# Splitting the first adaLN weight slabs by feature tile, and moving the second tile's loads, products and modulation

## The chip, the cores and the metric

The kernel runs on one core of one Trainium2 chip. Its time is the device time of one execution in microseconds (us), the median of several runs; the kernel before takes 650.75 us (three runs, 649.06 to 651.46). The profile is one more execution, taken by the hardware profiler, with a time of its own. Times in the text are counted from the start of the span, the stretch from the first to the last instruction.

## The reference, cut to what matters

One layer of a diffusion backbone on x (1024 tokens by 1024 features) with 256 context tokens:

```python
shift, scale, gate = adaln(c, w_ada, b_ada)          # silu(c) @ w_ada + b_ada, split in three
shift_c, scale_c, gate_c = adaln(c_ctx, w_ada, b_ada)
h = rmsnorm(x, norm_g) * (1 + scale) + shift
hc = rmsnorm(ctx, norm_g) * (1 + scale_c) + shift_c
q, k, v, za, u, bg, cg, zc = split(h @ w_in)          # w_in is 1024 x 4096
attn = neighbourhood_attention(q, k, v, kc, vc, rpb) * silu(za)
conv = gated_short_conv(u, bg, cg, zc)
out = x + gate * (concat(attn, conv) @ w_out)
```

The change concerns only the start: the two columns `silu(c)` and `silu(c_ctx)` times the shift and scale parts of `w_ada`, the normalisation of x, and the first products of h with `w_in` (three of the eight column groups, for the convolution).

## The kernel before, in words

**Tiles.** Features are cut into eight tiles of 128 (`KT` = 8, index k), tokens into eight tiles of 128 (index t) and two halves of four tiles each. A feature tile of h is kept transposed, features on partitions and 1024 tokens along the row, as a high and a low fp32r part (`hh[k]`, `hl[k]`). A product with full accuracy takes three matmuls: high by high, low weight by high, high weight by low.

**Order.** Up to the output stage the order of the instructions on each engine is written out by hand (`strict`): each engine, and SP's queue of loads too, runs its instructions in the order of the program text, and a waiting instruction holds up all behind it on the same engine.

**Loads at the start** (lines 527 to 555, all issued by SP). `load_slab(m, j)` loads the columns of `w_ada` for the two feature tiles 2m and 2m + 1; j = 0 is the shift part, j = 1 the scale part. A slab is 1 MB: 128 partitions by 8 rows of 256 numbers (1 KB runs). For m = 0 each of the two slabs comes as two DMAs of 512 KB. `load_x` loads token tiles of x, 512 KB each in 4 KB runs. `load_chunks` loads 192 KB of `w_in` for one feature tile k, in 512 byte runs. The order before is: slab (0,0), slab (0,1), x tiles 0 to 3, chunk 0, x tiles 4 to 7, chunk 1, slab (1,0), slab (1,1), chunks 2 and 3, slab (2,0). Later slabs share three buffers, so that a load can wait for a slab's last reader.

**Modulation.** `products(m, j)` (line 594) multiplies the two columns `c2` with a slab into a PSUM tile `tr`, two rows of 512 results; a plain fp32 matmul is two instructions in the trace. `row_copy` (ACT) brings the rows to SBUF, `modulation` (line 611) turns them to columns by tiny matmuls, and three small DVE operations make the shift and scale columns `ab`.

**Normalisation of x.** `square(t)` on ACT sums the squares of a token tile, `root(t)` is an addition on DVE and a power on POOL, `norm(t)` scales the tile on DVE. In the text `norm(t)` of one tile stands ahead of `root(t + 1)` or just behind it.

**From x to h.** `transposed(half, k)` (PE) turns the four token tiles of a half for feature tile k into one of two PSUM buffers `tr`; `turn(half, k, on)` (line 651) applies the modulation: ACT makes the high part, ACT or DVE the full value `hw`, DVE the low part. `split_chunk(k)` makes the high (ACT) and low (DVE) part of a chunk. `first_columns(half, k, part)` (line 670) is the product, nine matmuls of 512 columns in three parts: part 0 needs the high parts, part 1 the chunk's low part, part 2 h's low part. The accumulators `acc0[u][half]` take six PSUM banks and `tr` the other two.

**The order around the change** (lines 718 to 778): both slab products, the squares and norms of tiles 0 to 3, one modulation for feature tiles 0 and 1, the transposes of the first half for k = 0 and 1, `first_columns(0, 0)` and `(0, 1)` with the norms of tiles 4 to 7 beside them, half of `products(1, 0)`, `transposed(1, 0)`, the rest of `products(1, 0)`, `transposed(1, 1)`, `products(1, 1)`, `first_columns(1, 0)`, `row_copy(1)`, `transposed(0, 2)`, `modulation(1)`, `turn(0, 2)`, the splits of slab pair 2, `first_columns(1, 1)`; then a loop over m.

Of the kernel before, what the change touches and what calls it, by code (L numbers as in the profile page):

```python
# [19 lines left out]
P = 128  # L20
# [19 lines left out]
def body(tc, es, x, ctxt, w_ada, b_ada, w_in, q_g, k_g, rpbr, w_out, vecs, cst, out):  # L40
# [100 lines left out]
    def place(k, shape, dtype, name):  # L141

        return hpool.tile(shape, dtype, name=name, tag=f"h{k}")
# [377 lines left out]
    def tr():  # L521
        return ps0.tile([P, 512], F32, name="tr", tag="tr", bufs=2)
# [4 lines left out]
    def load_x(ts):  # L527
        for t in ts:
            xx[t] = xp.tile([P, D], F32, name="xx", tag="xx", bufs=8)
            sp.dma_start(xx[t], x[0, t * P:(t + 1) * P])  # L530

    def load_slab(m, j):

        new = place(6 + j, [P, KT, 256], F32, "slab") if m == 0 else sl.tile([P, KT, 256], F32, name="slab", tag="slab", bufs=3)
        n = 2 if m == 0 else 1
        for i in range(n):
            rows = slice(KT // n * i, KT // n * (i + 1))
            sp.dma_start(new[:, rows], bass.AP(w_ada.tensor, w_ada.offset + j * D + 256 * m + 3 * D * P * rows.start,
                                               [[3 * D, P], [3 * D * P, KT // n], [1, 256]]))
        slabs[m, j] = new  # L540

    def load_chunks(ks):
        for k in ks:
            chunks[k] = chunk_load(CU, k)

    load_slab(0, 0)
    load_slab(0, 1)
    load_x(range(4))
    load_chunks([0])
    load_x(range(4, 8))  # L550
    load_chunks([1])
    load_slab(1, 0)
    load_slab(1, 1)
    load_chunks([2, 3])
# [3 lines left out]
    for u, half in (0, 0), (2, 0), (0, 1), (2, 1), (1, 0), (1, 1):  # L558
        acc0[u][half] = ps0.tile([P, 512], F32, name=f"acc{u}{half}", tag=f"acc{u}{half}")

    pv = tr()
    pe.transpose(pv[:, :nvec], vec[:nvec], ident[:nvec, :nvec])
    dve.tensor_copy(vecT, pv[:, :nvec])
    act.activation(c2[:].rearrange("p k a -> p a k"), vecT[:, 0:16].rearrange("p (a k) -> p a k", a=2), AF.Silu)
# [7 lines left out]
    def square(xtile, n):  # L572

        sqj = cvp.tile([P, D], BF16, name="sqj", tag="cu", bufs=1)
        sums[n] = xp.tile([P, 1], F32, name="xss", tag="xss", bufs=4)
        act.activation(sqj, xtile, AF.Square, scale=1.0 / 32, accum_out=sums[n])

    def root(n):
        dve.tensor_scalar(sums[n], sums[n], EPS, None, ALU.add)
        pool.tensor_tensor(sums[n], sums[n], mhalf[:, 0:1], ALU.pow)  # L580

    def norm(xtile, n):
        dve.tensor_scalar(xtile, xtile, sums[n], None, ALU.mult)
# [10 lines left out]
    def products(m, j, kts=range(KT)):  # L594

        if m not in mods:
            mods[m] = tr()
        rows = mods[m][:2 if m < 2 else 4, 256 * j:256 * j + 256]
        parts = [(c2, slabs[m, j])] if m < 2 else [(c4, highs[j]), (c4, lows[j])]
        for i, (c, part) in enumerate(parts):  # L600
            for kt in kts:
                pe.matmul(rows, c[:, kt], part[:, kt], start=(i == 0 and kt == 0 and j == 0),
                          stop=(i == len(parts) - 1 and kt == KT - 1 and j == 1), skip_group_check=True)

    def row_copy(m):
        n = 2 if m < 2 else 4
        rw = cvp.tile([4, 512], F32, name="rw", tag="ub", bufs=2)
        act.copy(rw[:n], mods[m][:n])
        return rw[:n]

    def modulation(m, rw):

# [32 lines left out]
    def transposed(half, k, ts=range(4)):  # L645
        if (half, k) not in pts:
            pts[half, k] = tr()
        for i in ts:
            pe.transpose(pts[half, k][:, i * P:(i + 1) * P], xx[4 * half + i][:, k * P:(k + 1) * P], ident)

    def turn(half, k, on):

        modulated(rows_of(hh[k], half), rows_of(hl[k], half),
                  pts.pop((half, k))[:].rearrange("p (r b c) -> p r b c", r=8, b=8), k, 0, on)
# [58 lines left out]
    def split_chunk(k):  # L713
        chunks[k] = chunk_split(chunks[k])

    more_h(range(6))

    products(0, 0)
    products(0, 1)
    for t in range(4):  # L720
        square(xx[t], t)
    root(0)
    root(1)
    norm(xx[0], 0)
    root(2)
    norm(xx[1], 1)
    root(3)
    norm(xx[2], 2)
    rw = row_copy(0)
    modulation(0, rw)  # L730
    norm(xx[3], 3)
    transposed(0, 0)
    transposed(0, 1)
    square(xx[4], 4)
    root(4)
    split_chunk(0)
    turn(0, 0, dve)
    square(xx[5], 5)
    norm(xx[4], 4)
    root(5)  # L740
    turn(0, 1, dve)
    first_columns(0, 0)
    square(xx[6], 6)
    norm(xx[5], 5)
    root(6)
    square(xx[7], 7)
    norm(xx[6], 6)
    root(7)
    split_chunk(1)
    norm(xx[7], 7)  # L750
    first_columns(0, 1)
    products(1, 0, range(4))
    transposed(1, 0)
    turn(1, 0, act)
# [1 line left out]
    load_slab(2, 1)  # L756
    load_chunks([4, 5])
    transposed(1, 1)
    products(1, 1)
    load_slab(3, 0)  # L760
    split_chunk(2)
    turn(1, 1, act)
    first_columns(1, 0)
    rw = row_copy(1)
    split_chunk(3)
    split(2, 0, 0)
    load_slab(3, 1)
    load_chunks([6, 7])
    transposed(0, 2)
    modulation(1, rw)  # L770
    turn(0, 2, dve)
    split(2, 0, 1)
# [1 line left out]
    split(2, 1, 1)  # L774
    xc = sl.tile([P, 2, D], F32, name="xc", tag="slab", bufs=3)
    sp.dma_start(xc, ctxt[0].rearrange("(i p) d -> p i d", p=P))
    first_columns(1, 1)
    transposed(1, 2)

    for m in range(1, 4):  # L780
# [251 lines left out]
    def both(v, n, pair):  # L1032

        w = 256 if n % 4 == 0 else 384
        return v[:, pair[0][0]:pair[-1][0] + 1, :w]
# [387 lines left out]
```

## Time and profile before

| what | value |
|---|---|
| median of the runs (649.06 to 651.46) | 650.75 us |
| the profiled execution's own time | 651.68 us |
| its span | 649.9 us |
| mean granted TensorE clock | 0.994 |
| DVE busy | 431.9 us, 66% of the span |
| ACT busy | 322.6 us, 50% of the span |
| POOL busy | 129.4 us, 20% of the span |
| DMA traffic | 125.46 MB, 193 GB/s over the span |

The engines are PE (TensorE's matmuls), PEld (its weight loads), DVE (VectorE), ACT (ScalarE), POOL (GpSimd) and SP, which issues loads. The profile's page gives each engine's busy time, then the span in 40 slices (about 16 us each) with a busy digit in tenths. The chain of waits follows the work that ended last backwards, so that each piece of it held up the next. The timeline lists instructions as "start, duration, engine, line, operation, written tile <- read tiles, shape, count", with the idle time before it and what ended that in square brackets. Line 55 is the wrapper that records all instructions, so work is told apart by its tiles: `tr<-slab,c` are the slab products, `tr<-ci,rw` the modulation's tiny matmuls, `tr<-ci,xx` the transposes, `acc<-h,wh` and `acc<-h,wl` the matmuls of `first_columns`, `sqj<-xx` a square, `xss` the two steps of a root, `xx<-xx,xss` a norm, `h<-tr,ab` the high part in `turn`, `hw` its full value, `h<-hw,h` its low part.

### The profile page before, as it was taken

The numbers are of one execution on the slowest core, as the hardware profiler recorded it, in microseconds if no ns is written. First come the engines' busy times: TensorE is split into PE (matmuls) and PEld (weight loads), VectorE is DVE, ScalarE is ACT, GpSimd is POOL, SyncE is SP. The second block draws the span as 40 slices with busy tenths as digits, with TensorE's granted clock in tenths as the row PEclk, the third lists the DMA queues.
The fourth block names the chain that finished last, engine by engine and source line by source line (L and its number), as shares of the span: only waits on it lengthen the run. The fifth ranks groups of instructions, "written<-read, shape, count | busy, mean of one in ns | idle before, by whom it ended". The sixth has DMA issues, their size and how long they took to land.

```text
span 649.9 us, 10273 instructions
## 1 busy us (share of the span) xinstructions
PE 629.0 (97%) x3469; PEld 539.2 (83%) x3469; DVE 431.9 (66%) x814; ACT 322.6 (50%) x693; POOL 129.4 (20%) x137
## 2 busy tenths in 40 slices
PE   5799999999999999999999999999999999999997
PEld 1467799899899999977877888888888888888885
DVE  1557774966684856457786889988998864575111
ACT  3466653442553635428677558565685645352000
POOL 1203203312222132101121111111211111004321
PEclk9799999999999999999999999999999999999999
DMA  8854637686686898789939576886782223966521
GB/s 321 314 179 166 168 105 243 202 263 196 196 278 177 251 262 254 187 228 218 241 103 238 145 179 191 211 213 153 207 190 75 74 75 118 324 222 222 178 102 50
DMA packets 118864, 125.46 MB, mean 193 GB/s; under 512 B 32817, under 2 KB 89353, under 8 KB 117532
## 3 DMA queue, kind: packets, MB, share of 16 engines
q1 hardware_dynamic: 112348, 113.23, 60.9%
q10 hardware_dynamic: 6208, 11.05, 5.3%
q0 software_dynamic: 256, 0.54, 0.3%
q8 instruction: 27, 0.44, 0.3%
q14 instruction: 25, 0.20, 0.1%
HBM read 88.01 MB, written 38.53 MB: 195 GB/s over the span
## 4 chain that ended last, share of the span: by engine, by line
PE 72%; DMA 7%; DVE 7%; ACT 5%; SPq 4%; issue 2%; POOL 1%; ACTq 0%; DVEq 0%; POOLq 0%
PE pu L55 22%; PE pacc L55 17%; PE po L55 5%; PE pout L74 4%; PE pout L75 4%; PE pout L76 4%; SPq L55 3%; PE tr L55 3%; PE cacc L55 3%; PE pss L55 2%; PE pmx L55 2%; DMA v<-v_d 2%; DMA k_s<-k_d 2%; PE pc L55 2%; DVE mx L55 2%
## 5 line engine op out<-in xcount | busy, mean ns | idle before, releaser
L55 PE MATMUL pu<-h,uh 128*128 128x512 f32 x544 | 169.0, 392 | 0.0
L55 PE MATMUL pacc<-wh,h 128*128 128x384 f32 x512 | 135.1, 338 | 0.0
L55 PEld LDWEIGHTS pu<-h,uh 128*128 128x128 f32 x544 | 98.2, 188 | 17.0
L55 PE MATMUL pu<-h,ul 128*128 128x512 f32 x272 | 106.3, 391 | 0.0
L55 PEld LDWEIGHTS pacc<-wh,h 128*128 128x128 f32 x512 | 92.9, 188 | 0.1
L55 POOL TENSOR_TENSOR plc<-sc,phc 128x512 fp32r<-128x512 f32 x32 | 42.5, 1328 | 221.9 <-ACT sc L55 113.2
L55 PE MATMUL pacc<-wl,h 128*128 128x384 f32 x256 | 85.6, 335 | 0.0
L55 POOL TENSOR_TENSOR ss<-ss,few 128x4 f32<-128x4 f32 (+1 forms) x40 | 42.0, 1051 | 126.9 <-DVE ss L55 126.5
L55 PEld LDWEIGHTS pu<-h,ul 128*128 128x128 f32 x272 | 51.1, 188 | 11.2
L55 DVE TENSOR_TENSOR mx<-mx,sb 128x384 f32<-128x384 f32 (+1 forms) x64 | 55.1, 869 | 2.0
L75 PE MATMUL pout<-wol,yh 128*128 128x512 f32 x128 | 49.8, 389 | 0.0
L76 PE MATMUL pout<-woh,yl 128*128 128x512 f32 x128 | 49.6, 389 | 0.0
L74 PE MATMUL pout<-woh,yh 128*128 128x512 f32 x128 | 48.3, 389 | 0.0
L55 PEld LDWEIGHTS pacc<-wl,h 128*128 128x128 f32 x256 | 48.1, 188 | 0.1
L55 DVE TENSOR_REDUCE ss<-sq 128x4 f32<-128x260 f32 (+1 forms) x40 | 15.7, 393 | 46.0 <-ACT sq L55 45.0
L55 ACT COPY mg<-pmx 128x256 f32<-128x256 f32 x32 | 12.0, 374 | 57.8 <-PE pmx L55 47.2
L55 ACT ACTIVATE sq<-pacc 128x256 f32<-128x256 f32 x32 | 12.3, 386 | 53.1 <-PE pacc L55 52.3
L1355 DVE TENSOR_TENSOR ot<-pout,gate 128x512 f32<-128x512 f32 x16 | 10.8, 688 | 40.2 <-PE pout L76 37.7
L55 DVE TENSOR_TENSOR pll<-sb,phl 128x768 fp32r<-128x768 f32 (+2 forms) x33 | 29.3, 889 | 7.9 <-ACT sb L55 7.9
L1356 POOL TENSOR_TENSOR ot<-ot,xr 128x512 f32<-128x512 f32 x15 | 19.6, 1315 | 68.6 <-DVE ot L1355 67.6
L55 DVE TENSOR_TENSOR sc<-sc,mg 128x512 f32<-128x512 f32 x32 | 21.8, 683 | 17.1 <-ACT mg L55 17.1
L55 ACT ACTIVATE qn<-pacc,ss 128x64 f32<-128x64 f32 x128 | 30.1, 330 | 6.0 <-POOL ss L55 3.2
(146 smaller groups left out, 1276.0 us busy)
## 6 DMA issues: line engine op xcount, KB each, us to landing
uraw<-in_w_in SPq DMA_DIRECT2D x34, 256.0 KB
q_d<-qs SPq DMA_DIRECT2D x64, 128.0 KB
k_s<-k_d SPq DMA_DIRECT2D x16, 512.0 KB
q_s<-q_d SPq DMA_DIRECT2D x32, 256.0 KB
wr<-in_w_in SPq DMA_DIRECT2D x40, 192.0 KB
slab<-in_w_ada SPq DMA_DIRECT2D x6, 1024.0 KB
t_d<-btw SPq DMA_DIRECT2D x8, 576.0 KB
bt<-t_d SPq DMA_DIRECT2D x8, 576.0 KB
```

Source lines behind the costliest of these rows:

```text
L55: i = emit(*a, **kw)
L74: i = pe.matmul(ps, ah, bh, start=first, stop=False)
L75: pe.matmul(ps, ah, bl, start=False, stop=False)
L76: pe.matmul(ps, al, bh, start=False, stop=last)
L1355: dve.tensor_tensor(ot, ps, gate[:, cols], ALU.mult)
L1356: (dve if (nh, t) == (1, NB - 1) else pool).tensor_tensor(ot, ot, xr, ALU.add)
```

## The change

The slabs of feature tiles 0 and 1 are no longer one pair of 256 columns. `load_first_slabs(k)` loads, for one feature tile, the shift and the scale part as two DMAs of 512 KB in 512 byte runs. The pair of k = 0 stays first; x tiles 0 to 3 and chunk 0 follow; then the pair of k = 1, chunk 1, and x tiles 4 to 7.

`first_products(k, j)`, `first_row(k)` and `first_modulation(k)` do products, copy and modulation for one feature tile, into accumulator banks of the second half that are not yet in use (`acc0[1 - k][1]`) instead of `tr`; each plain fp32 matmul now has 128 columns instead of 256, and there are twice as many.

In the hand-written order the transposes of the first half are issued token tile by token tile. The products of k = 1 stand between the transposes of token tiles 2 and 3, and the modulation of k = 1 inside `first_columns(0, 0)`. `turn(0, 1)` follows there, with `split_chunk(1)` moved ahead of the squares of tiles 5 to 7 and of the norms of tiles 4 to 7. Further on, `products(1, 1)` with the load behind it moves behind `first_columns(1, 0)`, and part 0 of `first_columns(1, 1)` moves ahead of `modulation(1)`.

```diff
--- before.py
+++ after.py
@@ -531,24 +531,29 @@
 
     def load_slab(m, j):
 
-        new = place(6 + j, [P, KT, 256], F32, "slab") if m == 0 else sl.tile([P, KT, 256], F32, name="slab", tag="slab", bufs=3)
-        n = 2 if m == 0 else 1
-        for i in range(n):
-            rows = slice(KT // n * i, KT // n * (i + 1))
-            sp.dma_start(new[:, rows], bass.AP(w_ada.tensor, w_ada.offset + j * D + 256 * m + 3 * D * P * rows.start,
-                                               [[3 * D, P], [3 * D * P, KT // n], [1, 256]]))
+        new = sl.tile([P, KT, 256], F32, name="slab", tag="slab", bufs=3)
+        sp.dma_start(new, bass.AP(w_ada.tensor, w_ada.offset + j * D + 256 * m,
+                                  [[3 * D, P], [3 * D * P, KT], [1, 256]]))
         slabs[m, j] = new
+
+    def load_first_slabs(k):
+
+        both = place(6 + k, [P, 2, KT, P], F32, "slab")
+        for j in range(2):
+            sp.dma_start(both[:, j], bass.AP(w_ada.tensor, w_ada.offset + j * D + P * k,
+                                             [[3 * D, P], [3 * D * P, KT], [1, P]]))
+        slabs[k] = both
 
     def load_chunks(ks):
         for k in ks:
             chunks[k] = chunk_load(CU, k)
 
-    load_slab(0, 0)
-    load_slab(0, 1)
+    load_first_slabs(0)
     load_x(range(4))
     load_chunks([0])
+    load_first_slabs(1)
+    load_chunks([1])
     load_x(range(4, 8))
-    load_chunks([1])
     load_slab(1, 0)
     load_slab(1, 1)
     load_chunks([2, 3])
@@ -558,7 +563,7 @@
     for u, half in (0, 0), (2, 0), (0, 1), (2, 1), (1, 0), (1, 1):
         acc0[u][half] = ps0.tile([P, 512], F32, name=f"acc{u}{half}", tag=f"acc{u}{half}")
 
-    pv = tr()
+    pv = acc0[0][1]
     pe.transpose(pv[:, :nvec], vec[:nvec], ident[:nvec, :nvec])
     dve.tensor_copy(vecT, pv[:, :nvec])
     act.activation(c2[:].rearrange("p k a -> p a k"), vecT[:, 0:16].rearrange("p (a k) -> p a k", a=2), AF.Silu)
@@ -607,6 +612,30 @@
         rw = cvp.tile([4, 512], F32, name="rw", tag="ub", bufs=2)
         act.copy(rw[:n], mods[m][:n])
         return rw[:n]
+
+    def first_products(k, j):
+
+        ps = mods[k] = acc0[1 - k][1]
+        for kt in range(KT):
+            pe.matmul(ps[:2, P * j:P * j + P], c2[:, kt], slabs[k][:, j, kt], start=(j == 0 and kt == 0),
+                      stop=(j == 1 and kt == KT - 1), skip_group_check=True)
+
+    def first_row(k):
+        rw = cvp.tile([4, 512], F32, name="rw", tag="ub", bufs=2)
+        act.copy(rw[:2, :256], mods[k][:2, :256])
+        return rw[:2]
+
+    def first_modulation(k, rw):
+
+        pm = mods.pop(k)
+        for j in range(2):
+            pe.matmul(pm[:, 2 * j:2 * j + 2], rw[:, P * j:P * j + P], comb[:2], start=(j == 0), stop=(j == 1),
+                      skip_group_check=True)
+        both = lambda v: v[:, k:k + 1].broadcast_to([P, 2])
+        abk = ab[:, k].rearrange("p (w j) -> p j w", j=2)
+        dve.tensor_tensor(abk[:, 0], pm[:, 0:2], both(bsh), ALU.add)
+        dve.tensor_tensor(abk[:, 1], pm[:, 2:4], both(b1), ALU.add)
+        dve.tensor_tensor(abk[:, 1], abk[:, 1], both(ng), ALU.mult)
 
     def modulation(m, rw):
 
@@ -715,40 +744,54 @@
 
     more_h(range(6))
 
-    products(0, 0)
-    products(0, 1)
-    for t in range(4):
-        square(xx[t], t)
+    first_products(0, 0)
+    first_products(0, 1)
+    square(xx[0], 0)
     root(0)
+    square(xx[1], 1)
     root(1)
     norm(xx[0], 0)
+    transposed(0, 0, [0])
+    transposed(0, 1, [0])
+    square(xx[2], 2)
     root(2)
     norm(xx[1], 1)
+    rw = first_row(0)
+    first_modulation(0, rw)
+    transposed(0, 0, [1])
+    transposed(0, 1, [1])
+    square(xx[3], 3)
     root(3)
     norm(xx[2], 2)
-    rw = row_copy(0)
-    modulation(0, rw)
+    split_chunk(0)
     norm(xx[3], 3)
-    transposed(0, 0)
-    transposed(0, 1)
+    transposed(0, 0, [2])
+    transposed(0, 1, [2])
+    first_products(1, 0)
+    transposed(0, 0, [3])
+    turn(0, 0, dve)
+    transposed(0, 1, [3])
+    first_products(1, 1)
+    first_columns(0, 0, (0,))
+    rw = first_row(1)
     square(xx[4], 4)
     root(4)
-    split_chunk(0)
-    turn(0, 0, dve)
+    first_columns(0, 0, (1,))
+    first_modulation(1, rw)
+    first_columns(0, 0, (2,))
+    turn(0, 1, dve)
+    split_chunk(1)
     square(xx[5], 5)
     norm(xx[4], 4)
     root(5)
-    turn(0, 1, dve)
-    first_columns(0, 0)
     square(xx[6], 6)
     norm(xx[5], 5)
     root(6)
+    first_columns(0, 1)
     square(xx[7], 7)
     norm(xx[6], 6)
     root(7)
-    split_chunk(1)
     norm(xx[7], 7)
-    first_columns(0, 1)
     products(1, 0, range(4))
     transposed(1, 0)
     turn(1, 0, act)
@@ -756,17 +799,18 @@
     load_slab(2, 1)
     load_chunks([4, 5])
     transposed(1, 1)
-    products(1, 1)
-    load_slab(3, 0)
     split_chunk(2)
     turn(1, 1, act)
     first_columns(1, 0)
+    products(1, 1)
+    load_slab(3, 0)
     rw = row_copy(1)
     split_chunk(3)
     split(2, 0, 0)
     load_slab(3, 1)
     load_chunks([6, 7])
     transposed(0, 2)
+    first_columns(1, 1, (0,))
     modulation(1, rw)
     turn(0, 2, dve)
     split(2, 0, 1)
@@ -774,7 +818,7 @@
     split(2, 1, 1)
     xc = sl.tile([P, 2, D], F32, name="xc", tag="slab", bufs=3)
     sp.dma_start(xc, ctxt[0].rearrange("(i p) d -> p i d", p=P))
-    first_columns(1, 1)
+    first_columns(1, 1, (1, 2))
     transposed(1, 2)
 
     for m in range(1, 4):
```

## The prediction, as put on record before the result was known

> **What bounds the kernel now.** I read the page first, then the idle time at the start, because the change lies in the first 45 us.
>
> ```profile
> PE 629.0 (97%) x3469; PEld 539.2 (83%) x3469; DVE 431.9 (66%) x814; ACT 322.6 (50%) x693; POOL 129.4 (20%) x137
> ...
> PE   5799999999999999999999999999999999999997
> ```
>
> PE is busy 97% of the span, and its only poor slices are the first two, of some 16 us each. A change here can win little more than idle time of the first 32 us; what comes later follows PE. The next view is the table of stretches: start:end, length, busy time of PE, PEld, DVE, ACT and POOL, granted clock, DMA share, GB/s.
>
> ```profile
> 9.00:13.00 4.00, 4.00 (x18) 1.50 (x17) 0.15 (x1) 1.46 (x3) 0.18 (x1) 1.00 1.04 423
> 13.40:16.80 3.40, 1.65 (x8) 0.48 (x6) 2.16 (x6) 3.20 (x7) 2.29 (x3) 1.00 1.05 407
> 16.80:20.20 3.40, 2.29 (x16) 1.80 (x16) 1.95 (x7) 2.27 (x5) 1.50 (x2) 1.00 1.03 401
> 20.20:23.70 3.50, 3.38 (x8) 2.71 (x9) 3.33 (x6) 3.47 (x7) 0.55 (x1) 0.51 1.09 384
> 23.70:27.10 3.40, 1.78 (x6) 0.85 (x6) 2.31 (x6) 0.89 (x3) 1.23 (x2) 1.00 1.11 372
> 27.10:30.50 3.40, 3.40 (x9) 1.67 (x8) 0.75 (x1) 0.00 (x0) 0.05 (x1) 0.50 0.74 263
> 60.00:70.00 10.00, 10.00 (x68) 7.70 (x65) 7.25 (x10) 6.26 (x11) 7.31 (x8) 1.00 0.23 79
> 72.00:74.00 2.00, 2.00 (x12) 1.67 (x11) 0.75 (x2) 1.00 (x3) 0.00 (x0) 1.00 1.15 344
> ```
>
> Two things are to be seen. PE waits between 13.4 and 27.1 us, and it also runs at half clock twice, from 20.2 to 23.7 and from 27.1 to 30.5. Each half-clock stretch is about 3.4 us long and follows such a stretch with gaps (2.29 us busy, mostly transposes and tiny matmuls, and 1.78 us); but 1.65 us busy before 16.8 us cost nothing, so the edge is not sharp here. Loads run at 423 GB/s while x's 4 KB runs come, and at 344 with chunks alone (512 byte runs). The third view is the chain of waits (start, length, what held up the next).
>
> ```profile
> 26.80 2.70 PE acc L55 x6
> 29.50 8.87 PE tr L55 x40
> 38.37 2.28 PE acc L55 x9
> ...
> 43.41 2.83 ACT slabh L55 x3
> ...
> 47.64 2.03 PE tr L55 x16
> ```
>
> From 26.80 to 42 us PE's own work is the chain; then it goes through the modulation of the second slab pair, `turn(0, 2)`, three splits and `turn(1, 2)` on ACT to the products at 47.64, from where PE runs on without idle (10.00 of 10.00 us in the row of 60 to 70). So the change is worth what it moves **the start of that modulation**, the tiny matmuls at 41.02. The rest comes from rows of single instructions. First loads and products in the timeline of all engines:
>
> ```profile
> 6.02 9.03 PE L55 MATMUL tr<-slab,c 128*2 128x256 f32 x32 [2.44 <-DMA slab<-in_w_ada]
> ...
> 10.14 4.40 PEld L55 LDWEIGHTS tr<-slab,c 128*2 128x2 f32 x21 [0.20 <-issue]
> 11.33 1.06 ACT L55 ACTIVATE sqj<-xx 128x1024 bf16<-128x1024 f32 x1 [7.01 <-DMA xx<-in_x]
> ...
> 17.02 1.06 ACT L55 ACTIVATE sqj<-xx 128x1024 bf16<-128x1024 f32 x1 [0.26 <-DMA xx<-in_x]
> ```
>
> The slab products start as soon as the first piece of slab is there; tiles 0 and 4 of x are each waited for by their squares. Then PE's timeline where the second half begins and at the modulation:
>
> ```profile
> 31.76 0.66 PE L55 MATMUL tr<-ci,xx 128*128 128x128 f32 x4
> ...
> 41.02 1.05 PE L55 MATMUL tr<-ci,rw 2*128 2x2 f32 x8
> ```
>
> **The change part by part.**
>
> *Loads.* Bytes stay the same; 1.05 MB of slab moves behind x tiles 0 to 3 and chunk 0. The rate of 1 KB runs lies between 344 and 423 GB/s; I take 385, near the 384 of 20.2 to 23.7, when such slabs come. Tile 0 of x lands 1.05 MB earlier, 2.7 us, and loses 0.3 because the megabyte still ahead of it has 512 byte runs at 344: it lands at 11.33 - 2.4 = 8.9 us. Tile 4 landed at 17.02 behind 4.5 MB and half a megabyte of its own, so those 4.5 MB were in by 15.8; the same 4.5 MB now end with the second pair's scale slab: 15.8, plus 0.6 for 2.1 MB in short runs, is 16.4, and its shift slab is in 1.5 us before, at 14.9. Tile 4 lands at 18.2, behind chunk 1 too; slab (1,0) comes about 0.6 us later, long before its use. SP issues as many loads as before (four slab DMAs then, four now), and no issue waits for a buffer. [...]
>
> *First tile.* The views of single tiles give count, shortest, median and longest (ns), and first and last start:
>
> ```profile
> L55 ACT ACTIVATE sqj<-xx x8: 1046/1057/1058, 11.3 to 23.0; 128x1024 bf16<-128x1024 f32 x8
> L55 ACT ACTIVATION_READ_ACCUMULATOR sqj<-xx x8: 186/187/195, 12.3 to 24.0; 128x1 f32 x8
> ```
>
> ```profile
> L55 POOL TENSOR_TENSOR xss<-xss,few x8: 550/729/1032, 12.8 to 26.4; 128x1 f32<-128x1 f32 x8
> L55 DVE TENSOR_SCALAR xx<-xx,xss x8: 745/753/754, 14.0 to 27.2; 128x1024 f32<-128x1024 f32 x8
> ```
>
> ```profile
> L55 ACT COPY rw<-tr x3: 558/575/575, 16.2 to 53.6; 2x512 f32<-2x512 f32 x2, 4x512 f32<-4x512 f32 x1
> ```
>
> A square with its readout takes 1.25 us, so those of tiles 0 to 2 start at 8.9, 10.2 and 11.5. The row copy (0.57 us for 512 numbers; between nothing and 0.57 for 256, and I take 0.4) now stands ahead of square 3, which runs from 13.1 to 14.35. DVE's addition for tile 3 stands ahead of norm 2, so norm 2 (0.75) ends at 15.2; norm 3 waits for POOL's power (up to 1.03) and ends at 16.5. The first tile's modulation, its transposes and chunk 0's split fit between.
>
> *Second tile's products.* They cannot start before transposes of token tile 2, at 15.55. PE's queue is in order, so from here everything for feature tile 0 waits behind them too. One 256 column instruction took 0.21 us at full clock (4.40 us for 21), and 0.37 before (the first 11 in 4.1 us), so that the burst began at half clock. For 128 columns the bounds are half of that, 0.105, and no gain at all, 0.21; the transposes' 0.66 for four, 128 columns wide, put it near half, so I take 0.105. Two lots of 16 instructions are 3.4 us, with four transposes in between 0.3: at full clock the products end at **E = 19.3**, and the scale slab (16.4) is there in time. At half clock the 32 instructions take 6.8 us.
>
> *What follows E, at full clock.* DVE's timeline has the first tile's steps and the norms of tiles 5 and 6:
>
> ```profile
> 19.04 0.55 DVE L55 TENSOR_TENSOR wl<-wr,wh 128x384 fp32r<-128x384 f32 x1
> 20.30 0.81 DVE L55 TENSOR_SCALAR hw<-tr,ab 128x512 f32<-128x512 f32 x1 [0.71 <-ACT h L55]
> 21.14 0.69 DVE L55 TENSOR_TENSOR h<-hw,h 128x512 fp32r<-128x512 f32 x1
> ...
> 24.59 0.14 DVE L55 TENSOR_SCALAR xss<-xss 128x1 f32<-128x1 f32 x1
> 25.46 0.75 DVE L55 TENSOR_SCALAR xx<-xx,xss 128x1024 f32<-128x1024 f32 x1 [0.73 <-POOL xss L55]
> 26.13 0.15 DVE L55 TENSOR_SCALAR xss<-xss 128x1 f32<-128x1 f32 x1
> ```
>
> Row copy 0.4, beside it two parts of `first_columns(0, 0)` at 0.76 each (2.28 for nine matmuls), then half the tiny matmuls (0.55 of 1.05), three small DVE operations 0.5: the second tile's modulation is ready at E + 2.55. High part, full value and low part in `turn(0, 1)` take 2.3 us (ACT's 0.7 ahead of DVE in the bracket, then 20.30 to 21.83), chunk 1's low part 0.55. Only now come norms 4 to 7: norm 0.75, then three turns of addition, power and norm at 1.54 us each (24.59 to 26.13). Norm 7 thus ends at E + 10.8, and the second half's transposes start at E + 10.9. PE has too little to do meanwhile: its queue ends some 2.2 us before. **Here a new wait takes the old one's place**: before, the transposes at 31.76 waited for PE alone, since norm 7, the last of the norms, started at 27.2 and was over at 27.9; with E = 19.3 they start at 30.2, not earlier.
>
> *From there to the modulation.* Before: 41.02 - 31.76 = 9.26 us. `products(1, 1)` and `first_columns(1, 0)` only change places; part 0 of `first_columns(1, 1)` now lies ahead, 0.76, so 10.0. Behind the modulation the chain on ACT is the same, so that part 0 shortens nothing there but fills PE's wait. The moved load of slab (3,0) starts some 2 us later, behind `products(1, 1)`; its split comes after `turn(1, 2)`, around 48 us, which is cover enough for one megabyte.
>
> *Sum.* At full clock all through, the modulation starts at 19.3 + 10.9 + 10.0 = 40.2 against 41.02: **0.8 us gained**. But between 11.7 us (the first tile's products start at 6.0, run at half clock until 10.1 and at 0.105 us for the last 13) and 15.55 PE has only six transposes and four tiny matmuls. The rows above show half clock after such a stretch, and the next 3.4 us then fall on the second products: at most 1.7 us lost, 1.3 with an uneven fit, E = 20.6. The 2.2 us wait before the second half's transposes can do the same again, 1.7 us if it falls so; I count a quarter, 0.4. Then 41.9: **0.9 us lost**. On the profiled execution that is 651.7 + 0.9 = 652.6; the profile's execution lies 0.9 above the median shown, so beside the median the forecast is **651.6 us**.
>
> **The rivals.**
>
> 1. *The norms are not last* (faster). If DVE and POOL go through norms 4 to 7 sooner than 1.54 us each, PE bounds: it is through at E + 8.7, so 2.2 us earlier, and with full clock the modulation starts at 38.0, 3.0 us earlier: 647.7, a few tenths lower if the turns of `first_columns` close up as well. For it: POOL's powers took from 0.55 to 1.03 us for the same shape, so that part of a turn is loose. Against it: DVE's queue puts the norms behind chunk 1's split. Chance 0.12.
>
> 2. *Half clock nearly throughout* (slower). The place is 13 to 34 us; it decides once no 3.4 us stretch there has PE busy for more than about half. Price: 3.4 us on the products, 2.0 on `first_columns` and tiny matmuls ahead of the modulation's end, less what is already in the forecast, 1.7: 3.7 above it, 655.3. For it: products, then 0.9 and 2.2 us waits, look like 23.7 to 27.1 before, which lost the clock. Against it: the products themselves are dense, as those of 6 to 10 us, which ended at full clock. [...] Chance 0.18.
>
> 3. *The change does nothing*: loads are earlier, but the start waits for the second slab pair and the norms, and clock losses before and after are equal. 650.8, chance 0.10.
>
> **How the numbers follow.** The forecast has the other 0.60. A measurement of this kernel can tell about 0.5%, 3.25 us, from no change. Faster by more needs rival 1 with all its gain: 0.10. Slower by more is most of rival 2: 0.15. Within: 0.75. The range takes in all full clock with a little of rival 1, 648.2, up to just under rival 2, 655.0; about 0.1 is left out on either side. It also holds the unknown costs: 128 columns without gain (3.4 us, like half clock) and loads 0.5 us off.
>
> **What would show it.** Tile 0's square at 8.9 us (loads). The second products at 15.5 to 16 and their end at 19.3 or 20 to 21 with the clock row at half between (clock). Norm 7 ending 10.8 us behind that, PE idle before the second half's transposes at 30 to 32 (the new wait). The modulation of slab pair 1 at 40 to 42, the products behind it 6.6 us later, as before. I am wrong if those transposes come well before 30 us, or if PE idles again after 50 us where it did not.

## The result and the profile after

| | before | after |
|---|---|---|
| median of ten runs each on one chip | 650.39 us (649.06 to 652.26) | 654.97 us (652.21 to 657.92) |
| ratio, 95% interval | | 1.0063 (1.0045 to 1.008) |
| the profiled execution and its span | 651.68 us, 649.9 us | 656.41 us, 653.4 us |
| mean granted clock | 0.994 | 0.997 |
| products of slab pair 2 start | 47.64 us | 49.15 us |

The change costs 4.6 us where 0.9 was forecast. The time lies at the very edge of the range (655.0), and the sign is the forecast's, but most of the loss came from places that the prediction had called settled, so that the time lies in the range by luck. Two lines of the page of after:

```profile
PE 629.0 (96%) x3501; PEld 540.4 (83%) x3501; DVE 432.7 (66%) x817; ACT 322.9 (49%) x694; POOL 129.6 (20%) x137
...
PE   4899999999999999999999999999999999999997
```

PE's busy time is the same 629.0 us, in 32 matmuls and 32 weight loads more (3501 for 3469 each). So what the span has grown by is idle time of PE, and the digits don't show where. Mark the 64 instructions more; they matter below. The table of stretches of after (start:end, length, busy time of PE, PEld, DVE, ACT and POOL, granted clock, DMA share, GB/s):

```profile
5.40:10.40 5.00, 5.00 (x32) 3.18 (x32) 0.00 (x0) 0.93 (x1) 0.00 (x0) 1.00 0.98 356
10.40:12.80 2.40, 0.07 (x1) 0.00 (x0) 0.99 (x3) 2.19 (x5) 1.17 (x2) 1.00 1.04 383
12.80:15.20 2.40, 1.48 (x8) 0.92 (x8) 1.89 (x8) 2.03 (x6) 1.95 (x3) 1.00 1.15 346
15.20:18.60 3.40, 3.25 (x15) 1.91 (x16) 1.29 (x3) 0.00 (x0) 0.51 (x1) 0.50 1.08 403
18.60:22.00 3.40, 3.40 (x26) 2.29 (x25) 1.50 (x2) 1.39 (x3) 0.00 (x0) 1.00 1.03 405
60.00:70.00 10.00, 10.00 (x66) 7.85 (x65) 7.32 (x9) 5.80 (x10) 7.34 (x9) 1.00 0.04 19
76.00:78.00 2.00, 1.06 (x8) 0.70 (x6) 0.96 (x2) 1.63 (x4) 0.00 (x0) 1.00 0.52 150
```

Of these rows one is at half clock, 15.2 to 18.6, and it lies just on the first lot of the second products. PE is full at 60 to 70 us, as before. But at 76 to 78 it is busy for 1.06 of 2 us. That last row is the new thing. Then the start in PE's timeline of after:

```profile
5.37 5.10 PE L55 MATMUL acc<-slab,c 128*2 128x128 f32 x32 [1.84 <-DMA slab<-in_w_ada]
12.86 0.44 PE L55 MATMUL tr<-ci,xx 128*128 128x128 f32 x2 [2.39 <-DVE xx L55]
...
15.97 3.18 PE L55 MATMUL acc<-slab,c 128*2 128x128 f32 x16
...
19.45 1.91 PE L55 MATMUL acc<-slab,c 128*2 128x128 f32 x16
21.29 0.96 PE L55 MATMUL acc<-h,wh 128*128 128x512 f32 x3
...
30.27 0.66 PE L55 MATMUL tr<-ci,xx 128*128 128x128 f32 x3
32.14 0.33 PE L55 MATMUL tr<-ci,xx 128*128 128x128 f32 x1 [1.21 <-DVE xx L55]
...
41.69 1.05 PE L55 MATMUL tr<-ci,rw 2*128 2x2 f32 x8
...
49.15 1.09 PE L55 MATMUL tr<-slabh,c 128*4 128x256 f32 x8 [1.21 <-ACT hw L55]
```

The second products end at 21.3 (E), the modulation of slab pair 1 starts at 41.69 (41.02 before), and the products of slab pair 2 at 49.15 (47.64 before).

**Where the time went.** I matched the instructions of DVE and ACT in the two traces one by one and read the shift of each. It grows in steps: +0.67 us at the modulation, +0.84 between it and the products of slab pair 2, +1.35 near 72 us, +0.42 near 104, +0.25 near 345. That is 3.53 us, and the spans differ by 3.5. The rest of the two executions' 4.7 us lies outside the span (3.0 us against 1.8).

**The step of 0.84 us.** DVE's timeline, before and then after, around the three small operations (`ab`) that end the modulation:

```profile
40.38 1.22 DVE L55 TENSOR_TENSOR slabl<-slab,slabh 128x1024 fp32r<-128x1024 f32 x1 [0.39 <-ACT slabh L55]
42.10 0.16 DVE L55 TENSOR_TENSOR ab<-tr,vecT 128x4 f32<-128x4 f32 x1 [0.50 <-PE tr L55]
```

```profile
42.48 1.23 DVE L55 TENSOR_TENSOR slabl<-slab,slabh 128x1024 fp32r<-128x1024 f32 x1 [0.39 <-ACT slabh L55]
43.63 0.15 DVE L55 TENSOR_TENSOR ab<-tr,vecT 128x4 f32<-128x4 f32 x1
```

Before, the low part of a slab's split was over before the tiny matmuls were, and DVE waited 0.50 us for PE. After, it starts 2.1 us later, the `ab` operations stand behind it with no wait of their own, and they start 1.94 us behind the first tiny matmul instead of 1.08. The cause is one place further up: `products(1, 1)` ended at 38.4 and now ends at 40.5, ACT's row copy waits for it, and the splits behind the copy come later too. The row copy before and then after:

```profile
38.41 0.57 ACT L55 COPY rw<-tr 2x512 f32<-2x512 f32 x1 [2.10 <-PE tr L55]
```

```profile
40.52 0.58 ACT L55 COPY rw<-tr 2x512 f32<-2x512 f32 x1 [4.15 <-PE tr L55]
```

From the last `ab` operation to the products of slab pair 2 it is 5.27 us in both.

**The step of 1.35 us.** ACT's timeline at the loads of the query chunks, before and then after, and PE's of after:

```profile
72.96 1.06 ACT L55 CAST wh<-wr 128x384 fp32r<-128x384 f32 x2 [2.09 <-DMA wr<-in_w_in]
74.60 0.91 ACT L55 CAST wh<-wr 128x384 fp32r<-128x384 f32 x2
```

```profile
74.49 0.51 ACT L55 CAST wh<-wr 128x384 fp32r<-128x384 f32 x1 [2.12 <-DMA wr<-in_w_in]
76.37 0.51 ACT L55 CAST wh<-wr 128x384 fp32r<-128x384 f32 x1 [1.36 <-DMA wr<-in_w_in]
77.46 0.91 ACT L55 CAST wh<-wr 128x384 fp32r<-128x384 f32 x2
```

```profile
77.61 0.96 PE L55 MATMUL acc<-h,wh 128*128 128x512 f32 x3 [0.94 <-ACT h L55]
```

Before, two chunks are cast one right behind the other. After, the second waits 1.36 us for its load; the high part of the next `turn` stands behind it in ACT's queue, and PE waits for that. The chunks are loaded by the same instructions from the same place in both kernels, 192 KB each, far from anything that the diff touches. The DMA view (queue and kind: packets, MB, share of 16 engines) of two stretches of 7 us, each from 0.3 us behind the issue of the store `rope_d` that goes just ahead of these loads, before and then after:

```profile
DMA packets 2044, 1.99 MB, mean 284 GB/s; under 512 B 80, under 2 KB 1916, under 8 KB 1916
...
q1 hardware_dynamic: 2044, 1.99, 97.4%
```

```profile
DMA packets 1989, 1.98 MB, mean 283 GB/s; under 512 B 78, under 2 KB 1860, under 8 KB 1860
...
q1 hardware_dynamic: 1988, 1.96, 96.6%
q8 instruction: 1, 0.02, 0.8%
```

In after, an **instruction fetch** of 16 KB (q8) falls among the loads, and 56 packets fewer of the kernel's own queue (q1) come in the 7 us. The fetch took 0.89 us of one DMA engine. In before it comes at 79.05 us, when this burst is over. While the chunks come undisturbed, the DMA records of before have up to 352 packets in each half us (72.0 to 74.5 us), 336 to 338 of them of 512 bytes: 22 for each of 16 engines. If one engine alone lost the 56 packets, that is 1.27 us of its time, an estimate from these counts that lies near the step; the trace doesn't name the engine.

### The profile page after: what moved, and what is told of

It is laid out like the page before. It is cut to its first block, busy times and chain, and to the rows that moved or that the text cites. A ratio compares the mean times of both kernels' runs of the same rounds, so it can differ in the third digit from the quotient of the medians.

```text
span 653.4 us, 10342 instructions
## 1 busy us (share of the span) xinstructions
PE 629.0 (96%) x3501; PEld 540.4 (83%) x3501; DVE 432.7 (66%) x817; ACT 322.9 (49%) x694; POOL 129.6 (20%) x137
## 4 chain that ended last, share of the span: by engine, by line
PE 68%; DVE 9%; DMA 8%; SPq 3%; ACT 3%; issue 1%; POOL 1%; ACTq 0%; DVEq 0%; POOLq 0%
PE pu L55 20%; PE pacc L55 17%; PE po L55 5%; DMA k_s<-k_d 4%; PE pout L76 4%; PE pout L74 4%; PE pout L75 4%; PE cacc L55 3%; DVE mx L55 2%; SPq L55 2%; DVE sb L55 2%; PE pss L55 2%; PE tr L55 2%; PE pmx L55 2%; PE pc L55 1%
## 5 line engine op out<-in xcount | busy, mean ns | idle before, releaser
L55 PEld LDWEIGHTS pu<-h,ul 128*128 128x128 f32 x272 | 51.1, 188 | 11.3
L1399 DVE TENSOR_TENSOR ot<-pout,gate 128x512 f32<-128x512 f32 x16 | 10.8, 687 | 37.5 <-PE pout L76 33.2
```

What stands on the lines that cost most here:

```text
L55: i = emit(*a, **kw)
L1399: dve.tensor_tensor(ot, ps, gate[:, cols], ALU.mult)
```

## The experiments

Theory A: the loss is made at the start, by the late move of `products(1, 1)`, the wait for the norms and the clock, and what comes later follows from it or is chance. Theory B: a part is made near 72 us by something that the diff doesn't show, PE's instruction fetch, which comes earlier in the work because PE has 64 instructions more. The first eight runs split the loss among the parts; B took shape from their traces, where the step stayed whichever part was undone, and the last three runs test it. In the expectations of the first eight, theory B still says only that the later loss is a fixed consequence of the change, and in that of `norms_first` theory A is the wait for norm 7.

**The kernel after once more, and each part of the start by itself.** `after_again` is the kernel after unchanged.

> The changed kernel once more, unaltered. Theory A (the loss is made in two places: 1.5 us by the time of the products of slab pair 2, which began at 47.64 us before and at 49.15 after, and some 2 us later by single loads that land late, which differs from run to run): the first offset comes again within 1 us, depending on where the half-clock stretch falls; the second, 1.35 us at the load of the second query chunk near 75 us, comes out anywhere between 0 and 2 us. Theory B (the later loss is a fixed consequence of the change): the load near 75 us is late by 1.2 to 1.5 us again. Time by either: ratio to before 1.004 to 1.008.

Measured: 655.36 us, ratio 1.0067 (1.0044 to 1.009). The fourth transpose at 31.82, modulation 41.40, products of slab pair 2 at 48.85; the step near 72 us is 1.45. So the loss and both its places repeat.

`late_undone` puts the late moves back:

```diff
     transposed(1, 1)
+    products(1, 1)
+    load_slab(3, 0)
     split_chunk(2)
     turn(1, 1, act)
     first_columns(1, 0)
-    products(1, 1)
-    load_slab(3, 0)
...
-    first_columns(1, 1, (0,))
     modulation(1, rw)
...
-    first_columns(1, 1, (1, 2))
+    first_columns(1, 1)
```

> The changed kernel with its late part taken back: the products of slab (1,1) directly behind the transposes again, and the first product of the second half for feature tile 1 undivided behind the modulation. If part 0 ahead of the modulation costs its 0.76 us, the products of slab pair 2 start 0.8 us earlier than in the changed kernel relative to the second half's first transposes (17.0 us behind the fourth of them after; 16.2 expected here), and the time falls by about 0.8 us. If the late part is a gain, as filler for PE, they start no earlier or later. A loss that is all at the start leaves the time as in the changed kernel, 1.006.

Measured: 653.62 us, 1.0038 (1.0015 to 1.006). The products of slab pair 2 start 15.55 us behind the fourth transpose (17.01 in after, 16.2 expected). Of the 1.46 us, 0.61 lie ahead of the modulation and 0.85 behind it: the products follow it by 6.61 us, as before (6.62), and PE's wait ahead of them is back at 0.35 us. By the medians the late part is worth 1.7 us (2.87 above before, where `after_again` was 4.61 above it on the same chip), but the two intervals overlap. The step at 72 us is still 1.38, so the late part isn't what makes it. This profile has no stretch at half clock in the second products (1.91 us for each sixteen), though nothing ahead of them was changed, which may be why its start is earlier still (the products of slab pair 2 at 46.27).

`norms_first` keeps the diff and only moves the squares, roots and norms of tiles 4 to 7 up (the new places alone):

```diff
+    square(xx[4], 4)
+    root(4)
     turn(0, 0, dve)
...
+    square(xx[5], 5)
+    norm(xx[4], 4)
+    root(5)
     rw = first_row(1)
...
+    square(xx[6], 6)
+    norm(xx[5], 5)
+    root(6)
     turn(0, 1, dve)
     split_chunk(1)
+    square(xx[7], 7)
+    norm(xx[6], 6)
+    root(7)
     first_columns(0, 1)
     norm(xx[7], 7)
```

> The changed kernel with the squares and norms of token tiles 4 to 7 moved up: square 4 ahead of the first tile's turn, norm 4 ahead of the second tile's modulation, norm 5 ahead of the second turn, norms 6 and 7 behind it. Everything else as in the changed kernel. Theory A (norm 7, which ended at 32.08 us, holds up the second half's last transpose and PE waits for it): norm 7 ends near 29 us, PE goes through without a wait, the products of slab pair 2 start 1.4 us earlier, 47.7 us, ratio to before 1.003 to 1.006. Rival (the delayed second products and the half clock are all of it): norm 7 earlier, but those products no more than 0.5 us earlier.

Measured: 653.60 us, 1.0036 (1.0019 to 1.0054). Its PE timeline:

```profile
28.64 1.89 PE L55 MATMUL tr<-slab,c 128*2 128x256 f32 x8
30.46 0.66 PE L55 MATMUL tr<-ci,xx 128*128 128x128 f32 x4
```

All four transposes follow PE's own work with no bracket; the second products ran at half clock as in after (the first sixteen took 3.23 us, 3.18 in after). So the wait for norm 7 was real, and it cost 1.35 us at the modulation (40.34 against 41.69, one profile each). The step at 72 us stays, 1.42.

`pe_busy` is the kernel after with seven unread fp32 matmuls of 256 columns in PE's waits (five behind the first products, two ahead of square 3), meant to keep the clock.

> The changed kernel with seven extra plain fp32 matmuls of 256 columns whose results nothing reads, in PE's wait between the two bursts of slab products: five behind the first burst, two behind the transposes of token tile 1. If the half clock of 15.4 to 18.8 us comes from that wait, the granted clock stays at 1.0 there, the second burst ends at 19.6 instead of 21.3 us, norm 7 and the products of slab pair 2 come 1.5 us earlier, and the time falls by 1 to 1.5 us (ratio 1.004). If the clock falls from something else, it falls again, and the extra matmuls change nothing or cost up to 0.5 us.

Measured: 654.61 us, 1.0062 (1.004 to 1.0084). The clock stays at 1.00 up to the end of the second products, which end at 20.5 (19.6 expected); the fourth transpose is at 31.31, 0.8 us sooner than in after (1.5 expected). The step at 72 us is 0.7, and another, 1.4 us near 103, is larger than in after (0.42). The clock is worth 0.8 us at its place and nothing that the time can tell. All three kernels with the seven matmuls kept it here; of the profiles of the new start without them five lost it and one, `late_undone`, did not. So the matmuls are a likely reason and not a shown one.

**The late part alone, on the kernel before.** `before_again` is the kernel before unchanged, `late_alone` the same with the diff's late moves only (the last two hunks, from `products(1, 1)` on). Each was run once.

> The kernel before, unaltered, for a second profile. All five profiles with the changed start so far show a step against the first profile of before when the second query chunk is split, near 72 us (1.36, 1.47, 1.44, 1.40 and 0.73 us). Theory B (a fixed consequence of the change): this profile stays within 0.3 us of the first one there. Theory A (loads land early or late from run to run, and the first profile of before was an early one): a step of 0.7 to 1.5 us here too. The half-clock stretches may lie elsewhere in the first 35 us; the products of slab pair 2 begin between 46 and 48 us.

> The kernel before with the late part of the change alone: the products of slab (1,1) behind the first product of the second half for feature tile 0, and part 0 of that for feature tile 1 ahead of the modulation. The tiny matmuls of that modulation begin 10.0 us behind the second half's transposes instead of 9.26, and the products of slab pair 2 17.0 us behind them instead of 15.9 (within 0.3). If the late part is free, 15.9 again. At the load of the second query chunk: no step under theory B unless the late part is what causes it; 0 to 1.5 us under theory A.

Measured: 650.17 and 652.60 us. In `before_again` the transposes are at 30.33, the modulation at 39.58 and the products of slab pair 2 at 46.20: this start is 1.4 us ahead of the first profile of before. Its two stretches at half clock lie together, at 17.8 to 24.6, which may be why; no run tests it. In `late_alone` the modulation follows the transposes by 9.90 us (9.26 and 9.25 in the two profiles of before), and the products follow the modulation by 7.45 (6.62 in both). DVE's timeline of `late_alone` shows the same queue as that of after:

```profile
41.61 1.23 DVE L55 TENSOR_TENSOR slabl<-slab,slabh 128x1024 fp32r<-128x1024 f32 x1 [0.39 <-ACT slabh L55]
42.76 0.16 DVE L55 TENSOR_TENSOR ab<-tr,vecT 128x4 f32<-128x4 f32 x1
```

The late part costs 0.65 + 0.83 = 1.5 us by itself. Neither kernel has a step at 72 us (under 0.05 us in both).

**Parts together.** `both` is `norms_first` with the late moves put back; `all3` is that with the seven busy matmuls.

> The changed kernel with the norms moved up and the late part taken back. If both costs are real and add up, the products of slab pair 2 begin 0.8 us earlier than with the norms moved up alone (47.8), at 47.0 us with a half-clock stretch in the second products and near 45.5 without, so earlier than before (47.64). Time: ratio 1.000 to 1.004, since the later step near 72 us is not touched. If only one of the two costs is real, 47.6 or later and 1.004 or more.

> As the kernel with the norms moved up and the late part taken back, and the seven extra matmuls in PE's wait besides. Clock at 1.0 through 14 to 19 us in the profile, second burst over by 19.5 us, products of slab pair 2 at 45.5 us or a little before, 2 us earlier than in the kernel before. If the whole loss were at the start, that would make it faster than the kernel before by 2 us, ratio 0.997; if the loss of loads near 72 us is fixed, 0.998 to 1.001.

Measured: `both` 652.06 us, 1.0016 (0.9995 to 1.0036), with a step of 1.43 at 72 us; `all3` 651.89 us, 1.0016 (0.9991 to 1.004), with 0.17. The products of slab pair 2 start at 47.29 (47.0 expected, or 45.5 without a half-clock stretch; it had one of 6.8 us) and 45.97 (45.5 expected). With norms, late part and clock mended, the new start is only 0.2 us sooner than that of `before_again`, 46.20, so the early slabs win next to nothing there. In both, the second half's first transposes follow PE's own work without a wait (30.07 and 30.33 us).

**The fetch.** The trace's DMA records have the fetches of 16 KB one by one. By their number they are PE's: 27 in before and 28 in after for the 7039 and 7104 PE instructions of the trace, on average 250 apart, where each other engine has 1200 instructions or fewer in the whole span. The third one, and ACT's casts of the first two query chunks, in us behind the issue of the `rope_d` store:

| kernel | PE instructions more | third fetch | first cast | second cast | step at 72 us |
|---|---|---|---|---|---|
| before, before_again, late_alone | 0 | 11.74, 10.75, 11.33 | 5.65 to 5.69 | right behind | under 0.05 |
| after, after_again, late_undone | 64 | 5.42, 5.62, 5.47 | 5.67 to 5.68 | 7.56 to 7.68 | 1.35 to 1.45 |
| norms_first, both | 64 | 5.64, 5.59 | 5.68 to 5.69 | 7.65 to 7.66 | 1.42, 1.43 |
| pe_busy | 92 | 0.79 | 6.39 | right behind | 0.70 |
| all3 | 92 | 0.69 | 5.81 | right behind | 0.17 |

The step is there when the fetch falls between 5.4 and 5.7 us, and not when it falls after the burst; ahead of it, it is smaller or gone. But this was read after the fact, and most rows with the new start have the same count. So three more kernels move the fetch on purpose, by tiny fp32 matmuls of two columns that nobody reads (four instructions each), put into waits of PE at the start:

```diff
+    def tiny(n):
+        for i in range(n):
+            pe.matmul(acc0[2][1][:2, :2], c2[:, 0], c2[:, 1], start=True, stop=True, skip_group_check=True)
```

`before_64` is the kernel before with 16 of them, `after_60` the kernel after with 15, and `all3_32` is `all3` with eight. Their places in `before_64`:

```diff
+    tiny(6)
     products(0, 0)
     products(0, 1)
+    tiny(6)
...
-    first_columns(0, 1)
+    first_columns(0, 1, (0,))
+    tiny(4)
+    first_columns(0, 1, (1, 2))
```

> The kernel before, in its old order, with sixteen two-column fp32 matmuls that nobody reads put where PE waits anyway (six ahead of the slab products, six behind them, four between part 0 and part 1 of the second half's first columns). They are 64 instructions in PE's list, some 1 us of work. Theory of the instruction fetch: the third fetch of 16 KB comes 64 instructions sooner in the work, at 5.0 to 5.9 us behind the issue of the rope_d store, as in the kernel after, and not at 10.7 to 11.8; so ACT's cast of the second query chunk waits for its load, comes 1.8 to 2.1 us behind the first cast, and everything from 72 us on is 1.3 to 1.5 us later: time 1.0 to 2.0 us above before, a ratio of 1.002 to 1.003. Rival, that the 512-byte slab loads or the order of the norms make the late load: both are as in the kernel before, so no step at 72 us (under 0.1 us), and the time within 1 us of before.

Measured: 652.17 us against 651.71, 1.0016 (0.9988 to 1.0045). The fetch came 5.67 us behind the store. ACT's timeline and PE's:

```profile
71.50 0.51 ACT L55 CAST wh<-wr 128x384 fp32r<-128x384 f32 x1 [2.12 <-DMA wr<-in_w_in]
73.50 0.51 ACT L55 CAST wh<-wr 128x384 fp32r<-128x384 f32 x1 [1.49 <-DMA wr<-in_w_in]
```

```profile
74.74 0.96 PE L55 MATMUL acc<-h,wh 128*128 128x512 f32 x3 [1.06 <-ACT h L55]
```

The old order and the old loads, with 64 instructions more for PE, make the step: 1.46 us (shift against the first profile of before: -1.49 up to 68 us, -0.03 from 72). The rival expected none at that place. Nor is this an early start that a load gives back: `before_again` starts as early (-1.50 up to 68 us), its fetch comes after the burst, and its two casts stand together:

```profile
71.51 1.05 ACT L55 CAST wh<-wr 128x384 fp32r<-128x384 f32 x2 [2.14 <-DMA wr<-in_w_in]
```

> The kernel after with fifteen such matmuls (60 instructions: four ahead of the first slab products, eight behind them, three behind the first columns of the first half). Theory of the instruction fetch: the third fetch moves a further 60 instructions ahead, to before the query chunks' loads are asked for or less than 1 us behind the rope_d store; the cast of the second query chunk follows the first at once and the step at 72 us is under 0.3 us, while the start keeps its 0.7 to 1.5 us: time 1.0 to 2.0 us below after, a ratio of 1.003 to 1.005 against before. Rival, that the new order itself makes the load late: the step stays at 1.3 to 1.5 us and the time is that of after, a ratio of 1.006 to 1.007.

Measured: 655.22 us, 1.0051 (1.0025 to 1.0078). The fetch came 2.24 us ahead of the store. ACT's timeline:

```profile
74.37 1.06 ACT L55 CAST wh<-wr 128x384 fp32r<-128x384 f32 x2 [2.12 <-DMA wr<-in_w_in]
76.01 0.91 ACT L55 CAST wh<-wr 128x384 fp32r<-128x384 f32 x2
```

The two casts are together again and the step is under 0.05 us, with the start of after (products of slab pair 2 at 49.06). So theory B holds at its place, both ways. The times lean the same way and settle nothing: `before_64` is 0.5 us above before where 1.0 to 2.0 was expected, `after_60` 3.5 above where some 3.2 (4.6 less 1.4) was, and the intervals are wide enough for the rival too.

> The kernel with the late part undone, the norms ahead of the transposes and PE kept busy, and eight more two-column matmuls (32 instructions) in PE's waits at the start, so that the third fetch comes well before the query chunks' loads. Theory of the instruction fetch: no step at 72 us, the start 1.5 to 1.8 us ahead of the first profile of before; the later loads near 100 and 340 us may take back up to 2 us by where the further fetches fall: a ratio of 0.997 to 1.001. Rival, that the remainder is the 512-byte loads' own: as without the eight matmuls, 1.0016.

Measured: 651.84 us against 651.71, 0.9998 (0.9968 to 1.0028). The fetch came 1.57 us ahead of the store. No step at 72 us; the start is 1.7 us ahead of the first profile of before, and 1.4 of it is gone at 103 us. It is the best version of the new order, and no faster than the kernel before.

**What stays open.** The traces have more places where the shift jumps: at 103 us, where ACT waits for a load of `uraw` (11.3 to 13.5 us of idle time), and several between 320 and 385 us. The first runs from -0.6 to +1.6 us, the others together from -1.7 to +2.4, and the two profiles of before differ there as well (at 103 us by 1.4, which just takes back what `before_again` had won at the start). In `after_again` a stretch at half clock, 332.1 to 335.5, adds to it. By these numbers the uraw wait may swallow gains and losses made ahead of it, which would be a reason why 1.4 us at 72 us is hard to find in the time; no run here separated it. Why a fetch of 0.9 us makes a load 1.4 us late isn't settled either.

## Why the prediction was right up to the modulation and wrong behind it

- **Loads.** Tile 0's square at 9.47, forecast 8.9: the tile won 1.86 us instead of 2.4. The row of 12.80 to 15.20, when the packets are nearly all of 512 bytes (the second slabs and chunk 1), has 346 GB/s, against the 344 taken.
- **Second products.** Forecast 15.55 and E = 20.6 with a stretch at half clock; measured 15.97 and 21.3. The half-clock stretch came where it had been put. The first products ended at 10.5, where 11.7 was forecast; the forecast's own terms, 10.1 and 13 times 0.105, give 11.5. At full clock the last 16 instructions start 0.109 us apart (19.45 to 21.08), near the 0.105 taken; the start was 0.4 late. PE's longest gap ahead of the fall at 15.2 us was 2.39 us. In `after_again`, from the start of the first products on, no gap is over 0.66 us when the clock falls at 14.68 us, and in before the stretch of 16.8 to 20.2, just ahead of a half clock, has none over 0.79; so a gap of 2.39 us isn't needed. Nor does the second rival's measure, PE busy for about half of 3.4 us, decide it: in before the clock fell after 2.29 busy of 3.40 us (16.8 to 20.2) and stayed at 1.00 after 1.65 (13.4 to 16.8). What does decide it isn't shown.
- **Norm 7 at E + 10.8, and the new wait.** DVE's timeline of after:

```profile
26.70 0.75 DVE L55 TENSOR_SCALAR xx<-xx,xss 128x1024 f32<-128x1024 f32 x1
...
30.46 0.15 DVE L55 TENSOR_SCALAR xss<-xss 128x1 f32<-128x1 f32 x1
31.33 0.75 DVE L55 TENSOR_SCALAR xx<-xx,xss 128x1024 f32<-128x1024 f32 x1 [0.73 <-POOL xss L55]
```

  The last norm ends at 32.08, 10.8 us behind 21.3: right to a tenth, turn by turn (1.54 us). `norms_first` shows that it was the bound.
- **The modulation.** Forecast 41.9 in the likeliest case, measured 41.69. E was 0.7 later than forecast, and this was made good behind it: only the fourth transpose waited for norm 7, the first three began at 30.27, so that the modulation came 9.55 us behind the wait and not 10.0. No half clock came at 30 us, where 0.4 had been counted (granted clock 1.00 from 28 to 33 us).
- **First failed step: "Behind the modulation the chain on ACT is the same", the products 6.6 us behind.** They came 7.46 behind. ACT's chain itself is the same, 5.27 us from the last `ab` operation in both; what came later is those operations. I had asked what part 0 and the products do to PE and ACT, and not what the later row copy does to the splits and, through them, to DVE's queue, in which a low part of 1.23 us now stands ahead of three operations of 0.16. In `late_alone` the whole late part costs 1.5 us, where 0.76 was counted: the 0.65 ahead of the modulation had been foreseen, the 0.83 behind it had not.
- **Second failed step: from the products on, PE runs without idle and all is only shifted.** It idles at 77 us, for 1.35 us of shift, by the instruction fetch. This is what the prediction had named as the sign of being wrong. The forecast counted the instructions added to PE by their time, and they take almost none (629.0 us in both); their number moves the fetches (the third from 11.74 to 5.42 us behind the store).
- **The base.** The first profile of before had a start 1.4 us later than its repeat (47.64 against 46.20, and 46.16 in `before_64`); its second half's transposes, at 31.76, are the latest of the four profiles with the old start (30.29 to 30.93 in the others). The forecast was thus measured from a late start.
- **Rivals and chances.** No rival came true. A loss of more than 3.25 us had been given a chance of 0.15, as most of the second rival; it came by other causes. The time is close to the 655.3 us of the second rival, half clock nearly throughout, but the clock was at half for one stretch alone. A time that fits is no proof of a mechanism.

Together: the late part (1.5 us) and the wait for norm 7 (1.35) are about the 2.95 us by which the products of slab pair 2 come later in after, 49.15, than in `before_again`, 46.20; with the 1.35 to 1.45 of the fetch that is 4.3 to 4.4 us, near the 4.6 measured. Against the first profile of before the same sum gives 2.9 at 72 us. It holds to a microsecond or so at best, since the waits at 103 us and from 320 to 385 us take and give back as much. The times by themselves give most of the loss to the first two: `both`, which mends them and keeps the fetch's step, is only 0.84 us above before, and its interval (up to 1.0036) ends below that of `after_again` (from 1.0044). What the fetch adds to the whole time isn't shown: 0.5 us in `before_64` and 1.1 in `after_60`, neither clear of the noise.

## What to carry to other kernels

An edit that moves work by a microsecond must be followed through the queues of all engines that the moved work feeds, not only those of the engine that it is on: here a row copy on ACT that came 2 us later put a long operation of DVE ahead of three short ones. And when a step appears far from the edit, in code that didn't change, look at what else uses the DMA engines there; the number of instructions issued before that point, not their duration, can be what changed: here it was 64 PE instructions more, at the same 629.0 us of busy time. And a gain at one place may not last to the end: of what `before_again` had won at the start, 1.4 us was gone at the wait for `uraw` at 103 us, though it wasn't tested that this load takes it.

## What the runs showed of the hardware

- **Instruction fetches stand among the DMA records** (queue q8, kind `instruction`), in packets of 16 KB, one per some 250 PE instructions, 0.88 to 1.62 us each in before and after, 41 of 55 of them under 1.2. Where one fell 5.4 to 5.7 us behind the store, the work was 1.35 to 1.5 us late, in five kernels and one repeat; where it fell 0.7 to 0.8 us behind it, 0.17 and 0.7 us late, in two kernels; one that came over 1.5 us ahead of the store or 10 us behind it, in four kernels and one repeat, made no step: the second cast follows the first at once. A load beside the fetch came late, and moving the fetch brought that (`before_64`, 1.46 us) and took it away (`after_60`, under 0.05).
- **Time outside the span.** In all 83 runs of before that were made beside the experiments the time exceeds the span by 1.73 to 1.85 us. In the kernels with just 64 PE instructions more (after, `late_undone`, `norms_first`, `both`, `before_64`) 25 of 66 runs exceed it by 2.0 to 3.5 us, and none of the 48 runs of the kernels with 92 or 124 more. It isn't visible in the trace what happens there, but it goes with the instruction count and not with the order of the work: `before_64` has it too. In the ten runs of after it is 0.35 us more on average than in before (2.15 against 1.8), a part of the 4.6 that no sum of shifts holds.
- **The clock's stretches** at half clock near the start are 3.41 us long in the records of before and after, or 6.83 where two lie together (`before_again`), and their place differs from run to run of one kernel (17.8 to 24.6 in one profile of before; 20.3 to 23.7 and 27.1 to 30.5 in the other). The start differs by 1.4 us between these two; that the clock does it wasn't tested.
